# A third buffer for the second weight of a gate/up tile, queued for loading with the first

## The chip, the cores and the metric

The kernel runs on one core of one Trainium2 chip. Five engines work side by side, each through its own queue in order: TensorE (PE; its weight loads are shown apart as PEld), VectorE (DVE), ScalarE (ACT), GpSimd (POOL) and SyncE (SP), whose queue issues nearly all loads and stores. The metric is the device time in microseconds (us); lower is better.

## The reference

Two layers of an encoder on 512 tokens of width 1024: token mixing and memory attention, then a feed-forward part. The change is in the feed-forward part:

```python
h = rms_norm(x, g_ffn_pre[i])
gu = h @ w_gate_up[i]                       # 512 x 1024 by 1024 x 5632
f = (jax.nn.silu(gu[..., :D_FF]) * gu[..., D_FF:]) @ w_down[i]
x = x + rms_norm(f, g_ffn_post[i])
```

All of it is float32. D_FF is 2816.

## The kernel before

**Tiles and lots.** The gate/up product is worked in 22 tiles f = 0 to 21, each 128 columns of gate and the same 128 of up. `LOTS` cuts them into three lots: 0 to 7, 8 to 13, 14 to 21. After each lot the product with w_down for its tiles follows (`down`, after the third lot `ffn_out`). Tiles 0 and 1 are done in the plain way, the 20 others in seven products instead of eight, after Strassen's scheme in Winograd's form: sums of the activations' quarters (nS1, S2, S3, S4, made once) against sums of the weights.

**Weights of a tile.** A tile has two weights of 128 x 1024 float32, 512 KB each: raw (gate; pool `wraw`, 3 buffers, shared with all other weights) and rb (up; pool `gu`, 2 buffers). `prep_a` loads raw and splits it; `load_b` loads rb and makes two sums on VectorE: ru[:512] = raw[:512] + rb[:512] (L1043) and rb[:512] += rb[512:] (L1044). `prep_c` adds ru[512:] (L1049), `prep_d` adds to raw[512:] (L1056). Each of the four operands a (raw), c (ru), b (rb) and d (512 columns of raw) is then split into a high part on ScalarE (L313) and a low part on VectorE (L317), since each product is made of three matmuls of reduced precision. The 512-column split d is the last to read raw, so it frees the buffer for raw of tile f+3. The split b is the last to read rb, so it freed the buffer for rb of tile f+2.

**The order within a tile.** TensorE's order is written out by hand in `body(f)`: products with c (two), a of the next tile (first half), b (first half), a of the next tile (second half), b (second half), d. Each is 12 matmuls of 256 columns (L1065 to L1067). VectorE adds results that come back from the product banks: L1101 after the first b product, which must be done before the d product overwrites the bank; L1082 after the second a product; L1109 after the second b product; then L1115 and L1118 form the tile's output.

**The order on other engines.** Only TensorE's order is fixed by hand. For the other engines, and for the loads in SP's queue, a scheduler at build time takes instructions by their priority in the program and by the time at which it expects their inputs. Each engine then keeps that order on the chip, and waits at the head of its queue.

Of the kernel before, what the change touches and what calls it, by code (L numbers as in the profile page):

```python
# [9 lines left out]
F32 = mybir.dt.float32  # L10
# [6 lines left out]
P = 128  # L17
# [181 lines left out]
class Trunk:  # L199
# [791 lines left out]
    def ffn(self, l, pools, forms, late, done):  # L991
# [3 lines left out]
        nc = self.nc  # L995
        f32r = lambda pool, shape, tag, n=1: pool.tile(shape, F32R, tag=tag, name=tag, bufs=n)
        F, o, gu, tmp = {}, [], pools["gu"], None
        w, raw, st = {}, {}, {}

        def units(f):  # L1000
            w[f] = [self.unit(self.a["wgu"][l, f, b]) for b in range(2)]
# [23 lines left out]
        def pair(f, key, src, n=1024):  # L1025
            hi, lo = [self.whl.tile([P, 1024], F32R, tag=z, name=f"w{z}", bufs=4) for z in ("hi", "lo")]
            self.split(hi[:, :n], lo[:, :n], src)
            st[f][key] = (hi, lo)

        def prep_a(f):  # L1030
            st[f] = {}
            src = self.a["wgu"][l, f]
            ra = self.wraw.tile([P, 1024], F32, tag="raw", name="raw", bufs=3)
            nc.sync.dma_start(ra, src[0])
            raw[f] = ra
            pair(f, "a", ra)

        def load_b(f):
            src = self.a["wgu"][l, f]
            ru, rb = [gu.tile([P, 1024], F32, tag=z, name=z, bufs=2) for z in ("ru", "rb")]  # L1040
            nc.sync.dma_start(rb, src[1])
            with self.tc.issue_after(forms.last[1]) if f == 3 else nullcontext():
                nc.vector.tensor_add(ru[:, :512], raw[f][:, :512], rb[:, :512])  # L1043
                nc.vector.tensor_add(rb[:, :512], rb[:, :512], rb[:, 512:])  # L1044
            st[f].update(ru=ru, rb=rb)

        def prep_c(f):
            ru, rb = st[f]["ru"], st[f]["rb"]
# [36 lines left out]
        def body(f, pos, nxt, nxt2, fill):  # L1085
# [7 lines left out]
            if nxt is not None:  # L1093
                load_b(nxt)
                prep_c(nxt)
                p1(nxt)
            else:
                fill[0]()
# [7 lines left out]
            if nxt2 is not None:  # L1106
                prep_a(nxt2)
# [31 lines left out]
        for f in range(2):  # L1139
            for b in range(2):  # L1140
                plain(f, b, 1, pgs[f])
            act(f, pgs[f])
            if f == 0:
                forms.finish(0)
                prep_a(2)
                forms.finish(1)
        pools["forms"].close()

        for c, (f0, f1) in enumerate(LOTS):
            fs = list(range(f0, f1))  # L1150
# [2 lines left out]
            if c:  # L1153
                prep_a(gs[0])
            load_b(gs[0])
            prep_c(gs[0])
            prep_a(gs[1])
# [18 lines left out]
            if c < len(LOTS) - 1:  # L1176
                self.down(get, self.a["wd"][l], fs, c, o, head)
                if l == c == 0:
                    self.axial(gu.tile([P, 1024], F32, tag="ru", name="ru", bufs=2))
        done()  # L1180
        return get, fs, o, head

    def start(self, mkp):
# [215 lines left out]
```

## Time and profile before

| | us |
|---|---|
| median of 3 runs | 1095.49 |
| lowest, highest | 1094.43, 1097.13 |
| the profiled execution | 1097.01 |
| its span, first to last instruction | 1094.9 |
| TensorE busy | 1072.8 |
| VectorE busy | 840.8 |
| ScalarE busy | 659.1 |
| VectorE waits at L1043 for rb, for raw | 11.0, 12.0 |
| clock granted to TensorE (1 is full) | 0.998 |

A row of the timeline has the start (us from the span's start), the duration, the engine, the line, the operation, what it writes from what it reads, the count and, in brackets, the idle time before it and what ended that. "SPq" is a load or store issued by SP. A row of waits has the total, the number and the longest.

### The profile page before, as it was taken

The page shows a single profiled execution, that of the slowest core. Times are in us where ns is not written, and L with a number is a line of the kernel's source. Part 1 is how long each engine was busy: PE and PEld are TensorE (multiplying, and loading weights), DVE is VectorE, ACT ScalarE, POOL GpSimd, SP SyncE. Part 2 cuts the span into 40 slices and gives each one's busy share as a digit, 9 for nine tenths or more (in the row PEclk, how much of TensorE's full clock was granted, in tenths as well). Part 3 has the DMA queues.
Part 4 walks back from the last instruction along what each step waited for, and adds up shares of the span by engine and source line. Part 5 has one row for each costly group of instructions (what it writes and reads, how often), then busy time and mean ns, then how long its engine had stood idle before and what let it go on. Part 6 is the DMA issues. An engine that isn't in the chain of part 4 may idle for free.

```text
span 1094.9 us, 19518 instructions
## 1 busy us (share of the span) xinstructions
PE 1072.8 (98%) x7436; PEld 985.0 (90%) x7436; DVE 840.8 (77%) x1433; ACT 659.1 (60%) x1357; POOL 197.7 (18%) x341
## 2 busy tenths in 40 slices
PE   9999999999999999999999999999999999999997
PEld 7899878999889989998898888878999899899986
DVE  7889875999548867975888988758996478669854
ACT  7679874756445535653567888756664366346631
POOL 5773231102000000000444543312000000000001
PEclk9999999999999999999999999999999999999999
DMA  9621007344833472335533221144136123423243
GB/s 339 250 78 40 20 20 261 125 154 129 283 140 116 153 252 78 116 108 187 197 126 116 78 78 40 39 176 172 53 110 222 59 89 120 139 68 105 88 165 116
DMA packets 40702, 142.44 MB, mean 130 GB/s; under 512 B 4768, under 2 KB 5152, under 8 KB 40480
## 3 DMA queue, kind: packets, MB, share of 16 engines
q1 hardware_dynamic: 40320, 140.80, 37.4%
q8 instruction: 58, 0.95, 0.4%
q10 hardware_dynamic: 288, 0.40, 0.1%
q14 instruction: 36, 0.29, 0.1%
HBM read 122.30 MB, written 18.87 MB: 129 GB/s over the span
## 4 chain that ended last, share of the span: by engine, by line
PE 70%; DVE 5%; issue 2%; ACT 1%; POOL 1%; DMA 0%; DVEq 0%; POOLq 0%; ACTq 0%
PE ps L1065 11%; PE ps L1066 11%; PE ps L1067 11%; PE ps L304 10%; PE ps L303 10%; PE ps L305 10%; PE tp L668 2%; DVE wlo L317 1%; PE o L683 1%; PE o L682 1%; PE s L607 1%; PE s L608 1%; POOL r L337 1%; DVE hrows L317 1%; POOL p L658 0%
## 5 line engine op out<-in xcount | busy, mean ns | idle before, releaser
L313 ACT ACTIVATE whi<-raw 128x1024 fp32r<-128x1024 f32 (+3 forms) x206 | 169.2, 839 | 170.1 <-PE ps L1067 69.0
L317 DVE TENSOR_TENSOR wlo<-raw,whi 128x1024 fp32r<-128x1024 f32 (+3 forms) x202 | 191.0, 960 | 68.8 <-ACT whi L313 64.8
L1066 PE MATMUL ps<-hrows,wlo 128*128 128x256 f32 x640 | 176.4, 276 | 0.0
L1065 PE MATMUL ps<-hrows,whi 128*128 128x256 f32 x640 | 176.2, 275 | 0.0
L1067 PE MATMUL ps<-hrows,whi 128*128 128x256 f32 x640 | 176.2, 275 | 0.0
L303 PE MATMUL ps<-whi,hrows 128*128 128x256 f32 (+2 forms) x432 | 144.1, 333 | 0.0
L304 PE MATMUL ps<-wlo,hrows 128*128 128x256 f32 (+2 forms) x432 | 138.0, 320 | 1.6 <-DVE wlo L317 1.6
L304 PE MATMUL ps<-wlo,f 128*128 128x512 f32 (+1 forms) x360 | 138.6, 385 | 0.0
L303 PE MATMUL ps<-whi,f 128*128 128x512 f32 (+1 forms) x360 | 138.5, 385 | 0.0
L305 PE MATMUL ps<-whi,f 128*128 128x512 f32 (+1 forms) x360 | 138.5, 385 | 0.0
L305 PE MATMUL ps<-whi,hrows 128*128 128x256 f32 (+2 forms) x432 | 138.0, 320 | 0.0
L1065 PE MATMUL ps<-a,whi 128*128 128x256 f32 x480 | 132.3, 276 | 2.9 <-DVE c L1101 2.9
L1066 PE MATMUL ps<-a,wlo 128*128 128x256 f32 x480 | 132.1, 275 | 0.0
L1067 PE MATMUL ps<-a,whi 128*128 128x256 f32 x480 | 132.1, 275 | 0.0
L1066 PEld LDWEIGHTS ps<-hrows,wlo 128*128 128x128 f32 x640 | 120.1, 188 | 0.6
L1065 PEld LDWEIGHTS ps<-hrows,whi 128*128 128x128 f32 x640 | 120.1, 188 | 0.5
L1067 PEld LDWEIGHTS ps<-hrows,whi 128*128 128x128 f32 x640 | 120.1, 188 | 0.0
L346 POOL TENSOR_SCALAR e<-sso 128x1 f32<-128x1 f32 x8 | 3.4, 422 | 550.5 <-ACT junk L341 550.3
L658 POOL TENSOR_SCALAR p<-p,rd 128x256 f32<-128x256 f32 (+2 forms) x128 | 77.4, 623 | 102.5 <-DVE rd L655 62.3
L1065 PEld LDWEIGHTS ps<-a,whi 128*128 128x128 f32 x480 | 90.1, 188 | 3.5 <-DVE c L1101 3.3
L1066 PEld LDWEIGHTS ps<-a,wlo 128*128 128x128 f32 x480 | 90.1, 188 | 0.2
L1067 PEld LDWEIGHTS ps<-a,whi 128*128 128x128 f32 x480 | 90.1, 188 | 0.0
(201 smaller groups left out, 2551.0 us busy)
## 6 DMA issues: line engine op xcount, KB each, us to landing
raw<-in_wgu_dram SPq DMA_DIRECT2D x48, 512.0 KB, 4.4
raw<-in_wd_dram SPq DMA_DIRECT2D x44, 512.0 KB, 4.5
rb<-in_wgu_dram SPq DMA_DIRECT2D x40, 512.0 KB, 3.6
raw<-in_wo_dram SPq DMA_DIRECT2D x17, 512.0 KB, 4.1
raw<-in_wq_dram SPq DMA_DIRECT2D x16, 512.0 KB, 4.9
xt<-x SPq DMA_DIRECT2D x12, 512.0 KB, 4.9
raw<-in_wm_dram SPq DMA_DIRECT2D x8, 512.0 KB, 4.6
x<-y SPq DMA_DIRECT2D x8, 512.0 KB, 3.2
```

Source lines behind the costliest of these rows:

```text
L303: mm(out, lh, rh, start=first, stop=False)
L304: mm(out, lh, rl, start=False, stop=False)
L305: mm(out, ll, rh, start=False, stop=last)
L313: a = nc.scalar.activation(hi, src, AF.Copy)
L317: b = nc.vector.tensor_sub(lo, src, hi.bitcast(F32))
L337: g.tensor_tensor(r, r, self.mhalf[:, :r.shape[1]], op=OP.pow)
L607: nc.tensor.matmul(s[:, :n], qi, hd["ka"]()[:, k0 * P:k1 * P], start=True, stop=False)
L658: self.pooled = nc.gpsimd.tensor_scalar(hd["p"][z][:, :n], hd["p"][z][:, :n], rd[:, z:z + 1], 1.0, op0=OP.mult, op1=OP.mult)
L668: nc.tensor.transpose(tp[:, z], hd["p"][i][:, jj * P:(jj + 1) * P], self.ident)
L1065: mm(out, wh[:, s], rh, start=start and k == 0, stop=False, skip_group_check=True)
L1066: mm(out, wl[:, s], rh, start=False, stop=False, skip_group_check=True)
L1067: mm(out, wh[:, s], rl, start=False, stop=k == 3, skip_group_check=True)
```

## The change

The load of rb moves from `load_b` into `prep_a`, directly behind the load of raw. Every third tile, counted within a layer from tile 2, takes its rb from a new pool `gx` with one buffer, the others from `gu` as before, so there are three buffers in turn. The pool is opened when the temporary forms of the activations are closed, and closed at the end of the layer's last lot. The number and kind of instructions stay the same on each engine.

```diff
         F, o, gu, tmp = {}, [], pools["gu"], None
-        w, raw, st = {}, {}, {}
+        w, raw, st, turn, gx = {}, {}, {}, [-1], []
...
             raw[f] = ra
+            n = turn[0] = turn[0] + 1
+            rb = st[f]["rb"] = (gx[0] if n % 3 == 2 else gu).tile([P, 1024], F32, tag="rb", name="rb", bufs=1 if n % 3 == 2 else 2)
+            nc.sync.dma_start(rb, src[1])
             pair(f, "a", ra)
 
         def load_b(f):
-            src = self.a["wgu"][l, f]
-            ru, rb = [gu.tile([P, 1024], F32, tag=z, name=z, bufs=2) for z in ("ru", "rb")]
-            nc.sync.dma_start(rb, src[1])
+            ru, rb = gu.tile([P, 1024], F32, tag="ru", name="ru", bufs=2), st[f]["rb"]
             with self.tc.issue_after(forms.last[1]) if f == 3 else nullcontext():
                 nc.vector.tensor_add(ru[:, :512], raw[f][:, :512], rb[:, :512])
                 nc.vector.tensor_add(rb[:, :512], rb[:, :512], rb[:, 512:])
-            st[f].update(ru=ru, rb=rb)
+            st[f]["ru"] = ru
...
         pools["forms"].close()
+        extra = ExitStack()
+        gx.append(self.pool(extra, f"gx{l}"))
...
         done()
+        extra.close()
         return get, fs, o, head
```

TensorE's and GpSimd's orders are the same in both kernels; ScalarE's differs by one swap of neighbours in each layer. SP's and VectorE's differ at these places. In the new kernel lines from 1036 on stand one to four higher or lower: L1038 is the load of rb (L1041 before), L1044, L1045 and L1050 are the three sums (L1043, L1044 and L1049 before), L1057, L1083, L1102, L1110, L1116 and L1119 those that were L1056, L1082, L1101, L1109, L1115 and L1118. The numbers in names tell one tile's buffers from another's.

**SP at the start of layer 0's first lot**, before (raw_3305 and raw_3435 belong to tiles 3 and 4, rb_3511 to tile 4, rb_3641 to tile 5):

```order
L1034 DMA raw_3305<-in_wgu_dram 128x1024
L1034 DMA raw_3435<-in_wgu_dram 128x1024
L359 DMA gain_6460<-in_g_ffn_post_dram 128x1024
L359 DMA gain_6462<-in_g_mix_pre_dram 128x1024
L800 DMA xt_6644<-x00_74 128x1024
L800 DMA xt_6692<-x01_75 128x1024
L1041 DMA rb_3511<-in_wgu_dram 128x1024
L1034 DMA raw_3565<-in_wgu_dram 128x1024
L1041 DMA rb_3641<-in_wgu_dram 128x1024
```

The same place now (tile 4's rb is rb_3440, tile 5's is rb_3570, tile 6's is rb_3700):

```order
L1034 DMA raw_3308<-in_wgu_dram 128x1024
L1034 DMA raw_3438<-in_wgu_dram 128x1024
L1038 DMA rb_3440<-in_wgu_dram 128x1024
L1038 DMA rb_3570<-in_wgu_dram 128x1024
L1034 DMA raw_3568<-in_wgu_dram 128x1024
L1038 DMA rb_3700<-in_wgu_dram 128x1024
```

Each rb now stands one place of its kind earlier. The two gains and the two rows of x went to the end of layer 0's third lot, where the load of tile 21's rb stood; only there does the scheduler now find their memory free.

**VectorE in layer 0's first lot**, before: the sum of tile 5 (ru_3640), the split of tile 4's ru (ru_3510) and the result of tile 3 (c_3547), for which TensorE waits:

```order
L317 TENSOR_TENSOR wlo_3478<-raw_3305,whi_3477 128x512
L1044 TENSOR_TENSOR rb_3511<-rb_3511 128x512
L1118 SCALAR_TENSOR_TENSOR f12_3473<-s_3339,f02_3472 128x512
L1049 TENSOR_TENSOR ru_3510<-ru_3510,rb_3511 128x512
L1056 TENSOR_TENSOR raw_3435<-raw_3435,ru_3510 128x512
L1043 TENSOR_TENSOR ru_3640<-raw_3565,rb_3641 128x512
L317 TENSOR_TENSOR wlo_3517<-ru_3510,whi_3516 128x1024
L1101 TENSOR_TENSOR c_3547<-ps_3390,p5_3508 128x256
```

The same place now (tile 5's sum is ru_3645, tile 6's is ru_3775, tile 4's ru is ru_3515, tile 3's result is c_3550):

```order
L317 TENSOR_TENSOR wlo_3483<-raw_3308,whi_3482 128x512
L1050 TENSOR_TENSOR ru_3515<-ru_3515,rb_3440 128x512
L1119 SCALAR_TENSOR_TENSOR f12_3478<-s_3344,f02_3477 128x512
L1057 TENSOR_TENSOR raw_3438<-raw_3438,ru_3515 128x512
L317 TENSOR_TENSOR wlo_3520<-ru_3515,whi_3519 128x1024
L1044 TENSOR_TENSOR ru_3645<-raw_3568,rb_3570 128x512
L1102 TENSOR_TENSOR c_3550<-ps_3393,p5_3513 128x256
L1045 TENSOR_TENSOR rb_3570<-rb_3570 128x512
L1050 TENSOR_TENSOR ru_3645<-ru_3645,rb_3570 128x512
L1083 TENSOR_TENSOR s_3565<-ps_3552,p1_3536 128x256
L1044 TENSOR_TENSOR ru_3775<-raw_3698,rb_3700 128x512
```

The split of tile 4's ru went ahead of tile 5's sum, and tile 6's sum came forward into this tile's work.

**VectorE in layer 0's third lot**, before: from the 512-column split of tile 16 (raw_5527), which frees the buffer for raw of tile 19, to the sum of tile 18 (ru_5862):

```order
L317 TENSOR_TENSOR wlo_5700<-raw_5527,whi_5699 128x512
L1056 TENSOR_TENSOR raw_5657<-raw_5657,ru_5732 128x512
L1118 SCALAR_TENSOR_TENSOR f11_5695<-s_5524,f01_5694 128x512
L317 TENSOR_TENSOR wlo_5739<-ru_5732,whi_5738 128x1024
L1043 TENSOR_TENSOR ru_5862<-raw_5787,rb_5863 128x512
L1101 TENSOR_TENSOR c_5769<-ps_5612,p5_5730 128x256
```

The same place now, from the split of tile 16 (raw_5530) to the sum of tile 19 (ru_5997, from raw_5920):

```order
L317 TENSOR_TENSOR wlo_5705<-raw_5530,whi_5704 128x512
L1057 TENSOR_TENSOR raw_5660<-raw_5660,ru_5737 128x512
L1119 SCALAR_TENSOR_TENSOR f11_5700<-s_5527,f01_5699 128x512
L317 TENSOR_TENSOR wlo_5742<-ru_5737,whi_5741 128x1024
L1102 TENSOR_TENSOR c_5772<-ps_5615,p5_5735 128x256
L1044 TENSOR_TENSOR ru_5997<-raw_5920,rb_5922 128x512
```

The sum that stands behind tile 16's split is now that of tile 19, whose raw that split lets in; before it was that of tile 18. The result L1101 went ahead of it.

## The prediction

> **What bounds the kernel now.** I read the page's table of engines first, then the waits of TensorE, then the timelines of TensorE, VectorE and the load queue (SP) at the places those waits name.
>
> ```profile
> span 1094.9 us, 19518 instructions
> ...
> PE 1072.8 (98%) x7436; PEld 985.0 (90%) x7436; DVE 840.8 (77%) x1433; ACT 659.1 (60%) x1357; POOL 197.7 (18%) x341
> ```
>
> TensorE (PE) is busy for 98% of the span. Since a busy matmul may still be waiting inside its modelled duration, I look at a stretch of the gate/up work by itself, by windows; the columns are PE, weight loads, VectorE, ScalarE, GpSimd, clock, DMA share and GB/s:
>
> ```profile
> 418.00:490.00 72.00, 72.00 (x631) 71.72 (x630) 61.59 (x90) 44.64 (x75) 0.00 (x0) 1.00 0.33 107
> ```
>
> This is the third lot of layer 0. Weights are being loaded for 71.72 of 72 us, so there is nothing to win there: the loads already come in time for TensorE. VectorE works 61.59 of 72 us. Over the whole run, TensorE waits in a gate/up tile only here (total, times, longest):
>
> ```profile
> PE ps L1065 <- DVE c L1101: 2.9, 2, 2.3
> ```
>
> The two waits in TensorE's timeline, one in the first lot of each layer:
>
> ```profile
> 242.34 0.28 PE L1067 MATMUL ps<-hrows,whi 128*128 128x256 f32 x1
> 244.88 0.39 PE L1065 MATMUL ps<-a,whi 128*128 128x256 f32 x1 [2.27 <-DVE c L1101]
> ...
> 796.48 0.28 PE L1067 MATMUL ps<-hrows,whi 128*128 128x256 f32 x1
> 797.43 0.38 PE L1065 MATMUL ps<-a,whi 128*128 128x256 f32 x1 [0.67 <-DVE c L1101]
> ```
>
> Matmuls of this shape start 0.11 us apart, so 2.43 us are lost at 244.88 and 0.84 at 797.43: **3.3 us in all**. That is what a better supply of weights can bring.
>
> **What the change removes.** VectorE before the first wait, and the load queue:
>
> ```profile
> 229.03 0.69 DVE L1043 TENSOR_TENSOR ru<-raw,rb 128x512 f32<-128x512 f32 x1
> ...
> 239.86 0.69 DVE L1049 TENSOR_TENSOR ru<-ru,rb 128x512 f32<-128x512 f32 x1
> ...
> 242.66 0.69 DVE L1043 TENSOR_TENSOR ru<-raw,rb 128x512 f32<-128x512 f32 x1 [1.39 <-DMA rb<-in_wgu_dram]
> 243.28 1.22 DVE L317 TENSOR_TENSOR wlo<-ru,whi 128x1024 fp32r<-128x1024 f32 x1
> 244.41 0.42 DVE L1101 TENSOR_TENSOR c<-ps,p 128x256 f32<-128x256 f32 x1
> ```
>
> ```profile
> 220.83 0.33 SPq L359 DMA_DIRECT2D gain<-in_g_ffn_post_dram  x1
> ...
> 228.57 0.33 SPq L1041 DMA_DIRECT2D rb<-in_wgu_dram  x1
> ...
> 237.56 0.33 SPq L1041 DMA_DIRECT2D rb<-in_wgu_dram  x1
> ```
>
> The addition at 242.66 belongs to tile 5. It stands at the head of VectorE's queue and waits 1.39 us for rb of tile 5, asked for at 237.56 and landed 5.1 us later. Behind it stand the split of tile 4's ru and the addition L1101, for which TensorE waits. With the third buffer, rb of tile 4 is asked for directly behind raw of tile 4, ahead of the place where the gain load stood (220.83), and rb of tile 5 takes the place at 228.57. So this wait is gone.
>
> **What is late next in that lot** is VectorE itself. Spacings come from a steady tile of the third lot:
>
> ```profile
> 452.13 0.68 DVE L1043 TENSOR_TENSOR ru<-raw,rb 128x512 f32<-128x512 f32 x1
> 452.73 0.42 DVE L1101 TENSOR_TENSOR c<-ps,p 128x256 f32<-128x256 f32 x1
> 453.07 0.68 DVE L1044 TENSOR_TENSOR rb<-rb 128x512 f32<-128x512 f32 x1
> 453.67 0.69 DVE L1049 TENSOR_TENSOR ru<-ru,rb 128x512 f32<-128x512 f32 x1
> 454.27 0.42 DVE L1082 TENSOR_TENSOR s<-ps,p 128x256 f32<-128x256 f32 x1
> 454.80 1.23 DVE L317 TENSOR_TENSOR wlo<-raw,whi 128x1024 fp32r<-128x1024 f32 x1
> 455.94 0.42 DVE L1109 TENSOR_TENSOR c<-ps,u 128x256 f32<-128x256 f32 x1
> 456.28 1.22 DVE L317 TENSOR_TENSOR wlo<-rb,whi 128x1024 fp32r<-128x1024 f32 x1
> 457.41 0.69 DVE L1115 TENSOR_TENSOR s<-s,c 128x512 f32<-128x512 f32 x1
> 458.01 0.69 DVE L317 TENSOR_TENSOR wlo<-raw,whi 128x512 fp32r<-128x512 f32 x1
> ```
>
> So one start follows the next after 0.60 us for 512 columns, 0.33 for 256 and 1.13 for a split of 1024. From the addition of tile 3 (229.03, unmoved) to L1101 of tile 3, the new order has 13 operations of 512 columns, 3 of 256 and 4 of 1024: 7.8 + 1.0 + 4.5 = 13.3 us. L1101 starts at about 242.4, ends 0.42 later, and TensorE goes on at about 242.9, 2.0 us earlier than before. It could have gone on at 242.45, so 0.45 us of the stall stay. The next tile brings a small one: from L1101 of tile 3 to that of tile 4 stand 9 operations of 512, 3 of 256 and 3 of 1024, 5.4 + 1.0 + 3.4 = 9.8 us, against 9.5 us of matmuls (below), since additions of later tiles now stand earlier. That costs 0.3. **Gain in layer 0: 1.7 us.** The same count in layer 1:
>
> ```profile
> 782.95 0.68 DVE L1043 TENSOR_TENSOR ru<-raw,rb 128x512 f32<-128x512 f32 x1
> ...
> 796.96 0.42 DVE L1101 TENSOR_TENSOR c<-ps,p 128x256 f32<-128x256 f32 x1
> ```
>
> 782.95 + 13.3 = 796.25 instead of 796.96, so 0.7 us, less the same 0.3: **gain in layer 1: 0.4 us.** Together 2.1; the ends are 3.3 (no stall stays) and 1.0 (each stall that stays is half a microsecond longer than counted).
>
> **What the change adds.** It adds no instruction; every load and every addition is there as often as before. But VectorE's order moves: the addition L1043 of a tile now stands nearly one tile earlier, right behind the split that frees the buffer for its other input. That input is raw, the first weight, which keeps its three buffers: raw of tile f is asked for when the 512-column split of tile f-3 has read the buffer. Before, that split was followed by a whole tile of work ahead of the addition that needs the new raw; now four instructions lie between. Three loads of the third lot before:
>
> ```profile
> 419.78 0.33 SPq L1034 DMA_DIRECT2D raw<-in_wgu_dram  x1
> ...
> 448.00 0.33 SPq L1041 DMA_DIRECT2D rb<-in_wgu_dram  x1
> 449.21 0.33 SPq L1034 DMA_DIRECT2D raw<-in_wgu_dram  x1
> ...
> 458.73 0.33 SPq L1034 DMA_DIRECT2D raw<-in_wgu_dram  x1
> ```
>
> The landing times of the five such loads in this lot, then of those in the same lot of layer 1:
>
> ```profile
> DMA to landing us min/median/max: 4.1/4.4/4.4
> ```
>
> ```profile
> DMA to landing us min/median/max: 4.2/4.4/6.1
> ```
>
> A tile takes 9.52 us (449.21 to 458.73). The new circle is: L1043 of tile f, then L1044, L1082, L1049, the raw split, L1109, the rb split, L1115 and the 512-column split (0.60 + 0.60 + 0.33 + 0.60 + 1.13 + 0.33 + 1.13 + 0.60 + 0.69 = 6.0 us), then the issue and the landing of raw of tile f+1 (4.35), then L1043 of tile f+1: **10.4 us, against 9.52.** So VectorE falls behind by 0.9 us a tile while the circle lasts, from tile 17 to tile 21. L1043 of tile 17 goes as soon as its raw lands, at 419.78 + 4.4 = 424.2; L1101 comes between in the first round, so tile 21's goes at 424.2 + 10.7 + 3 x 10.4 = 466.1. Behind it come L1044, L1082, L1049 (with itself 2.1 us) and then the split of raw of tile 20, done 1.23 later, at 469.5. Before, that split and the matmul that needs it:
>
> ```profile
> 464.32 1.22 DVE L317 TENSOR_TENSOR wlo<-raw,whi 128x1024 fp32r<-128x1024 f32 x1
> ```
>
> ```profile
> 468.58 0.28 PE L1066 MATMUL ps<-a,wlo 128*128 128x256 f32 x1
> ```
>
> There was a slack of 3.0 us; now the matmul waits 0.9. After tile 21 no addition of this kind follows and VectorE catches up. With landings of 4.1 the stall is 0; with 4.4 it is 1.1; with one landing of 6.1, as once in layer 1, it is 2.8. I take 0.9 in layer 0 and 1.1 in layer 1, near the medians: **loss 2.0.** The first and second lots have only two rounds of the circle each and end before the slack is used up: I count 0, at most 0.4 each.
>
> **What else moves.** In layer 0 the gain vectors and two rows of x for the end of the feed-forward are loaded at the end of the third lot, where the last rb load stood, and not at 220.83.
>
> ```profile
> 467.04 0.33 SPq L1041 DMA_DIRECT2D rb<-in_wgu_dram  x1
> ```
>
> ```profile
> 512.01 0.69 DVE L940 TENSOR_TENSOR o<-o,gain 128x512 f32<-128x512 f32 x1 [0.19 <-ACT junk L341]
> ```
>
> The first use of a gain is 45 us after that place, so four loads cost nothing unless they hold up w_down's loads behind them. Those wait for VectorE to free raw buffers anyhow.
>
> **Two rules of the Trainium skill.** Its page "Perfetto Trace Analysis", section "Optimization Strategy", says that the same gap coming back on the engine that should be saturated can mean too few buffers for the next tile; by that rule alone the third buffer would win the whole 3.3 us. The rows here show two gaps and no recurring one, so the rule hardly fits. Its page "DMA: Bandwidth & Descriptors", section "Rules for kernel authors", advises to issue a load early and to wait for it late, by which the change would also gain 3.3 us. The order of instructions here does only half of it: rb is issued a tile earlier, and VectorE's wait for both weights moves a tile earlier too.
>
> **The sum.** -2.1 + 2.0 = -0.1 us. The profiled execution took 1097.01 us, 1.5 above the median of 1095.49 (its span, 1094.9, leaves 2.1 outside); the sum is taken off the median: **1095.4 us**. About 3.3 us (0.3%) is what a measurement of this kernel can tell from no change.
>
> **The rivals.**
> - All stalls go and none comes: raw lands in 4.1 us or less, and VectorE's order costs nothing. 1095.5 - 3.3 = 1092.2. For it: one raw landed in 4.1. Against: the medians, and VectorE's 13.3 us of queued work in the first lot. Chance 0.12, half of it beyond 0.3%. The two rules of the Trainium skill above, "Optimization Strategy" of "Perfetto Trace Analysis" and "Rules for kernel authors" of "DMA: Bandwidth & Descriptors", lead to this rival.
> - The circle through raw becomes the bound: in both layers raw lands later than 4.4, since the deeper rb load runs beside it. It decides from 4.2 us on and costs four steps of the excess in each third lot. At 5.0 us the step is 11.05, tile 21's addition is 2.6 us later than counted, and the stall is 3.5 us in each layer: 7.0 - 2.1 = +4.9, 1100.4; at 4.7 it is +2.5. For it: one landing of 6.1. Against: an rb load starts 1.2 us ahead of the raw load in each tile before (448.00 and 449.21) and after alike. Chance 0.16, most of it beyond 0.3%.
> - The change does not do what it says, the third buffer being held by its earlier tenants: 1095.5. Against: the order has that load directly behind the raw loads. Chance 0.06.
> - The forecast, within 2.5 us of the median either way: 0.66.
>
> So faster by over 0.3%: 0.06, within 0.3%: 0.80, slower: 0.14. The range from 1092.4 to 1099.0 takes in the first rival and part of the second.
>
> **What would show it.** The additions L1043 of the whole run, with their idle time at the end:
>
> ```profile
> L1043 DVE TENSOR_TENSOR ru<-raw,rb 128x512 f32<-128x512 f32 x40 | 27.5, 687 | 23.1 <-DMA raw<-in_wgu_dram 12.0 <-DMA rb<-in_wgu_dram 11.0
> ```
>
> Right: the wait of L1065 for L1101 at 244.88 falls from 2.3 to below 0.6 us; VectorE's L1043 waits for raw and no longer for rb (its waits before stand at the end of the row above), in the third lots by about 1 to 1.5 us a tile; TensorE shows a new wait near 468 for the split of raw, about 1 us. Wrong: no new wait there, which means that raw landed sooner; or a wait in each tile from 440 on, which means that the slack was smaller; or a wait for a gain or a w_down split after 470.

## The result, and the profile after

| | us |
|---|---|
| the changed kernel, median of 4 runs | 1104.38 |
| lowest, highest | 1103.61, 1104.91 |
| the old kernel beside it, median of 4 runs | 1096.31 |
| ratio, 95% interval | 1.0073 [1.0053, 1.0093] |
| the profiled execution, its span | 1104.53, 1102.4 |

The changed kernel is slower by 0.7%, about 8 us; 1095.4 was forecast, and the time lies above the range. Two executions of the experiments took far longer than the others of their kernels, 2176.94 us in e1, where it was the profiled one, and 1181.25 us in e6, and the ratios leave them out. The page of the changed kernel: the span, the busy time of the engines, then the chain that ended last, by engine and by line.

```profile
span 1102.4 us, 19508 instructions
...
PE 1077.4 (98%) x7436; PEld 987.8 (90%) x7436; DVE 841.4 (76%) x1433; ACT 655.5 (59%) x1357; POOL 195.7 (18%) x341
...
PE 80%; DVE 9%; ACT 4%; DMA 3%; issue 2%; POOL 2%; DVEq 0%; POOLq 0%; ACTq 0%
PE ps L304 13%; PE ps L303 13%; PE ps L305 13%; PE ps L1067 10%; PE ps L1066 10%; PE ps L1068 9%; PE tp L668 3%; DMA raw<-in_wgu_dram 3%; DVE wlo L317 2%; PE o L682 2%; PE o L683 2%; PE s L607 1%; PE s L608 1%; PE ps L513 1%; DVE mT L331 1%
```

The work is the same (7436 matmuls, 1433 VectorE instructions), the span is 7.5 us longer, and a load of raw now stands in the chain. Since TensorE's instructions are the same in the same order, the time from one of them to another can be compared by their starts. A lot below runs from the first matmul of its first product in seven parts to the first matmul of the w_down product behind it; the 12 matmuls of w_down within the last tile count with the lot. The third lot of layer 0 in the changed kernel, its first and last row in TensorE's timeline:

```profile
412.66 0.28 PE L1066 MATMUL ps<-a,whi 128*128 128x256 f32 x1
...
495.94 0.39 PE L303 MATMUL ps<-whi,f 128*128 128x512 f32 x1
```

That is 83.28 us. The same for all stretches, in us, with three kernels of the experiments beside it (the first stretch starts at the first matmul):

| stretch | old | changed | changed, second profile | e1: sums late | e2: four raw | e5: first lots only |
|---|---|---|---|---|---|---|
| up to the first lot | 220.8 | 219.2 | 219.6 | 219.4 | 219.7 | 219.6 |
| layer 0, first lot | 62.61 | 61.07 | 61.28 | 61.01 | 60.90 | 61.13 |
| layer 0, second lot | 60.00 | 60.40 | 60.55 | 60.03 | 59.99 | 60.00 |
| layer 0, third lot | 79.09 | 83.28 | 81.94 | 79.07 | 79.27 | 79.03 |
| between the layers | 281.5 | 281.9 | 281.8 | 281.7 | 281.4 | 281.8 |
| layer 1, first lot | 61.24 | 61.05 | 61.36 | 60.99 | 60.89 | 61.03 |
| layer 1, second lot | 60.01 | 61.91 | 62.33 | 60.03 | 60.05 | 60.00 |
| layer 1, third lot | 79.05 | 82.82 | 83.45 | 79.07 | 79.07 | 79.03 |

The w_down products between the lots take 40.83 and 29.95 us in each of these profiles. So the first lots gained 1.54 + 0.19 = 1.7 us, and the second and third lots lost 0.4 + 4.2 + 1.9 + 3.8 = 10.3. The rest (-1.6 ahead of the first lot, +0.4 between the layers, +0.2 behind the last lot) lies in work that the change doesn't touch. The first stretch varies by itself: in e3, whose queues have the old kernel's order, it took 219.2.

The waits of the changed kernel that answer to those of before (total, times, longest):

```profile
DVE ru L1044 <- DMA raw<-in_wgu_dram: 40.0, 23, 4.7
...
PE ps L1067 <- DVE wlo L317: 5.4, 7, 2.0
...
PEld ps L1066 <- DVE c L1102: 0.7, 4, 0.2
```

VectorE's sum (L1043 before, L1044 now) waits for raw 23 times, 40.0 us in all, and no longer for rb. TensorE's matmuls no longer wait for the result c (only weight loads still do, 0.7 us in all), and a wait for a split has come. One round of VectorE in the third lot of layer 0, from one sum to the next:

```profile
432.68 0.69 DVE L1044 TENSOR_TENSOR ru<-raw,rb 128x512 f32<-128x512 f32 x1 [1.62 <-DMA raw<-in_wgu_dram]
433.41 0.69 DVE L1045 TENSOR_TENSOR rb<-rb 128x512 f32<-128x512 f32 x1
...
438.15 0.69 DVE L317 TENSOR_TENSOR wlo<-raw,whi 128x512 fp32r<-128x512 f32 x1
...
441.30 0.42 DVE L1102 TENSOR_TENSOR c<-ps,p 128x256 f32<-128x256 f32 x1
443.44 0.69 DVE L1044 TENSOR_TENSOR ru<-raw,rb 128x512 f32<-128x512 f32 x1 [1.72 <-DMA raw<-in_wgu_dram]
...
455.50 0.69 DVE L1044 TENSOR_TENSOR ru<-raw,rb 128x512 f32<-128x512 f32 x1 [3.02 <-DMA raw<-in_wgu_dram]
...
466.15 0.69 DVE L1044 TENSOR_TENSOR ru<-raw,rb 128x512 f32<-128x512 f32 x1 [1.61 <-DMA raw<-in_wgu_dram]
```

The loads of raw in SP's queue in the same stretch:

```profile
438.87 0.33 SPq L1034 DMA_DIRECT2D raw<-in_wgu_dram  x1
...
449.63 0.33 SPq L1034 DMA_DIRECT2D raw<-in_wgu_dram  x1
...
461.68 0.33 SPq L1034 DMA_DIRECT2D raw<-in_wgu_dram  x1
```

The circle of the prediction can be read off: the sum at 432.68, the split that frees the buffer at 438.15 (ends 438.84), the load at 438.87, the next sum at 443.44. That is 6.19 us of VectorE and 4.57 of load, 10.76 in all, against TensorE's 9.52. The round behind it takes 12.06, because that load, issued at 449.63, serves its sum only at 455.50. The chain of waits goes through the same circle near the end of the lot (its rows have start, duration, what), and a round earlier, behind the late load, stands TensorE's longest stall of the lot:

```profile
460.37 0.69 DVE s L1116
461.06 0.61 DVE wlo L317
461.68 4.35 DMA raw<-in_wgu_dram
466.15 0.70 DVE ru L1044
...
468.51 1.15 DVE wlo L317
469.70 0.39 PE ps L1067
```

```profile
459.04 0.39 PE L1067 MATMUL ps<-a,wlo 128*128 128x256 f32 x1 [1.98 <-DVE wlo L317]
...
469.70 0.39 PE L1067 MATMUL ps<-a,wlo 128*128 128x256 f32 x1 [0.59 <-DVE wlo L317]
```

### The profile page after: what moved, and what is told of

It is laid out like the page before. It is cut to its first block, busy times and chain, and to the rows that moved or that the text cites. A ratio compares the mean times of both kernels' runs of the same rounds, so it can differ in the third digit from the quotient of the medians.

```text
span 1102.4 us, 19508 instructions
## 1 busy us (share of the span) xinstructions
PE 1077.4 (98%) x7436; PEld 987.8 (90%) x7436; DVE 841.4 (76%) x1433; ACT 655.5 (59%) x1357; POOL 195.7 (18%) x341
## 4 chain that ended last, share of the span: by engine, by line
PE 80%; DVE 9%; ACT 4%; DMA 3%; issue 2%; POOL 2%; DVEq 0%; POOLq 0%; ACTq 0%
PE ps L304 13%; PE ps L303 13%; PE ps L305 13%; PE ps L1067 10%; PE ps L1066 10%; PE ps L1068 9%; PE tp L668 3%; DMA raw<-in_wgu_dram 3%; DVE wlo L317 2%; PE o L682 2%; PE o L683 2%; PE s L607 1%; PE s L608 1%; PE ps L513 1%; DVE mT L331 1%
## 5 line engine op out<-in xcount | busy, mean ns | idle before, releaser
L1067 PE MATMUL ps<-hrows,wlo 128*128 128x256 f32 x640 | 177.6, 277 | 0.0
L1067 PE MATMUL ps<-a,wlo 128*128 128x256 f32 x480 | 133.6, 278 | 5.5 <-DVE wlo L317 5.4
L1067 PEld LDWEIGHTS ps<-hrows,wlo 128*128 128x128 f32 x640 | 120.2, 188 | 0.8 <-DVE wlo L317 0.2
L1067 PEld LDWEIGHTS ps<-a,wlo 128*128 128x128 f32 x480 | 90.2, 188 | 7.2 <-DVE wlo L317 7.0
```

What stands on the lines that cost most here:

```text
L1067: mm(out, wl[:, s], rh, start=False, stop=False, skip_group_check=True)
```

## The experiments

Theory A: the loss comes from the early sum at the head of VectorE's queue, which waits for raw, and raw waits for a buffer that VectorE itself frees. Against it stand B (the loads, queued together or moved, cost by themselves) and D (the early sums crowd VectorE, whatever they wait for). In the experiments' timelines the sum is L1045, one line lower, unless said otherwise. Ratios are to the old kernel, run on the same chip in the same session.

**e1, the sums in their old place, the loads in their new one.** An ordering edge keeps a tile's first sum behind the split of the tile before's ru:

```diff
-            self.split(hi[:, :n], lo[:, :n], src)
+            st[f][key + "lo"] = self.split(hi[:, :n], lo[:, :n], src)[1]
...
+            prev = st.get(f - 1, {}).get("clo")
-            with self.tc.issue_after(forms.last[1]) if f == 3 else nullcontext():
+            with self.tc.issue_after(forms.last[1]) if f == 3 else self.tc.issue_after(prev) if prev is not None else nullcontext():
```

> The changed kernel with one edit: the sum ru[:512] = raw[:512] + rb[:512] of a tile is ordered behind the split of the tile before's ru, where the old kernel has it. The load queue keeps the new order in every row, the third buffer stays. Theory A (VectorE's head of queue: the sum stands a tile early and waits for raw, which comes only after its own circle): the waits for raw split in the third lots and in layer 1's second lot go (lot times back to 79.1, 60.0 and 79.05 us from 83.3, 61.9 and 82.8), the gain of 1.5 us in layer 0's first lot stays; about 1094.5 us, 10 below the changed kernel. Theory B (the load queue: rb loaded earlier runs beside raw and delays it, or the moved gain and x rows do): nothing but the wait at the sum changes, the third lots stay near 83 us and the time near 1104.

Measured: 1094.2 us, ratio 0.9976 [0.9968, 0.9985]. B falls: SP's order is the changed kernel's in every row, and the loss is gone. A second run of this kernel gave the profile that is compared here:

> The changed kernel with the sums in their old place once more, for its profile. Theory A: third lots 79.1 us, second lots 60.0, first lot of layer 0 61.0 to 61.3; VectorE's waits for raw at the sum as few as in the old kernel (7 or fewer, 12 us or less, against 23 and 40), while rb and raw are loaded in the new order and raw's landing stays near 4.4 us. Theory B: raw's landing is what costs, and third lots above 81 us show it in this profile too.

It took 1093.8 us, and its stretches stand in the table. The waits in its profile:

```profile
DVE ru L1045 <- DMA raw<-in_wgu_dram: 9.3, 4, 3.6
```

A load, and the sums after it, in its third lot of layer 0 (SP, then VectorE):

```profile
436.69 0.33 SPq L1034 DMA_DIRECT2D raw<-in_wgu_dram  x1
```

```profile
439.62 0.68 DVE L1045 TENSOR_TENSOR ru<-raw,rb 128x512 f32<-128x512 f32 x1
...
449.14 0.68 DVE L1045 TENSOR_TENSOR ru<-raw,rb 128x512 f32<-128x512 f32 x1
```

The sums are 9.52 us apart again and wait for nothing. The load at 436.69 is that of the next tile: it has until 449.14, 12.45 us, where in the changed kernel the sum that needs it is the next one, four instructions behind. Raw lands hardly faster than in the changed kernel: over the sixteen loads of the second and third lots of both layers it takes 4.50 us on average in this profile, 4.65 in the changed kernel and 4.53 in the old one. It is waited for later.

**e2, a fourth buffer for raw, the sums still early.**

```diff
-            ra = self.wraw.tile([P, 1024], F32, tag="raw", name="raw", bufs=3)
+            n = turn[0] = turn[0] + 1
+            q = n % 4 == 3
+            ra = (gx[1] if q else self.wraw).tile([P, 1024], F32, tag="raw", name="raw", bufs=1 if q else 3)
...
-            n = turn[0] = turn[0] + 1
...
-        gx.append(self.pool(extra, f"gx{l}"))
+        gx.extend(self.pool(extra, f"gx{z}{l}") for z in range(2))
```

> The changed kernel with a fourth buffer for raw in the gate/up tiles, in turn; sums stay a tile early. Theory A (the circle from the 512-column split through the issue and landing of raw to the next sum): raw is now asked for a tile (9.5 us) earlier, the circle has 19 us for two tiles, and VectorE's waits for raw in the third lots fall from 1.5 to 4.6 us a tile to under 0.5; third lots near 79.2 us, about 1094 to 1096 us. Theory D (not the wait: the early sums push VectorE's splits and results back by their own 1.8 us a tile): the third lots stay above 81 us and the time above 1100.

Measured: 1093.33 us, ratio 0.9965 [0.9954, 0.9977], below what either theory expected and the lowest ratio of all, though its interval overlaps those of e1 and e9. Three rows of its third lot, a load of raw and two sums:

```profile
427.48 0.33 SPq L1036 DMA_DIRECT2D raw<-in_wgu_dram  x1
```

```profile
430.53 0.69 DVE L1045 TENSOR_TENSOR ru<-raw,rb 128x512 f32<-128x512 f32 x1
...
440.04 0.69 DVE L1045 TENSOR_TENSOR ru<-raw,rb 128x512 f32<-128x512 f32 x1
```

The load at 427.48 is for the sum at 440.04, a whole tile later than in the changed kernel, and no sum of the third lots' rounds waits, though each still stands a tile early. The early place alone costs nothing, which goes against D; what the changed kernel lacks is raw in time.

**e5, the new form in the first lots only.** Tiles 8 to 21 load rb in `load_b`, into the two old buffers.

```diff
-            rb = st[f]["rb"] = (gx[0] if n % 3 == 2 else gu).tile([P, 1024], F32, tag="rb", name="rb", bufs=1 if n % 3 == 2 else 2)
-            nc.sync.dma_start(rb, src[1])
+            if f < 8:
+                rb = st[f]["rb"] = (gx[0] if n % 3 == 2 else gu).tile([P, 1024], F32, tag="rb", name="rb", bufs=1 if n % 3 == 2 else 2)
+                nc.sync.dma_start(rb, src[1])
...
-            ru, rb = gu.tile([P, 1024], F32, tag="ru", name="ru", bufs=2), st[f]["rb"]
+            ru = gu.tile([P, 1024], F32, tag="ru", name="ru", bufs=2)
+            if f < 8:
+                rb = st[f]["rb"]
+            else:
+                rb = st[f]["rb"] = gu.tile([P, 1024], F32, tag="rb", name="rb", bufs=2)
+                nc.sync.dma_start(rb, self.a["wgu"][l, f][1])
```

> The changed kernel with the new form (third buffer, rb asked for with raw) in the first lot of each layer only; tiles 8 to 21 load rb in the old place into the two old buffers. Theory A: first lots as in the changed kernel (61.1 us each), second and third lots as before (60.0, 79.1); 1096.3 - 1.7 = about 1094.5. Theory B' (the loss in the third lots is set by what stands ahead of them, such as the pool held open through the layer or the moved loads of gains and x rows): the third lots stay above 81 us although their own tiles are unchanged, about 1101.

Measured: 1094.82 us, ratio 0.9984 [0.9976, 0.9993]. The gain of the first lots stays and the later lots are as before, though the pool is open through the whole layer and the gain vectors are loaded in another place.

**The changed kernel once more.**

> The changed kernel once more, for a second profile beside these runs. Theory A: the same lots lose (third lots of both layers, second lot of layer 1), rounds of VectorE's sum from 10.6 us up, each set by 6.2 us of VectorE's work plus the landing of raw; which tile loses most moves with single landings of 5 to 6 us. Chance alone (the first profile had two odd landings): third lots near 80 to 81 us and about 1098.

Measured: 1105.6 us, ratio 1.008 [1.0063, 1.0098]. The same four lots lose (10.1 us together, table). In layer 0's third lot no load came late this time, its rounds took 10.56 to 11.14 us, and it still lost 2.9 us, where it had lost 4.2. Layer 1's second and third lots lost more than in the first profile.

**e10, the extra buffer given to raw alone.** The old kernel with a fourth raw buffer and two of rb:

```diff
-            ra = self.wraw.tile([P, 1024], F32, tag="raw", name="raw", bufs=3)
+            n = turn[0] = turn[0] + 1
+            q = n % 4 == 3
+            ra = (gx[0] if q else self.wraw).tile([P, 1024], F32, tag="raw", name="raw", bufs=1 if q else 3)
...
+        extra = ExitStack()
+        gx.append(self.pool(extra, f"gx{l}"))
...
+        extra.close()
```

> The old kernel with the extra buffer given to raw (a fourth) and none to rb; the sums stay in their old place in the second and third lots but for three of them. Theory A: nothing early waits, so nothing is lost (third lots 79.1, second lots 60.0); rb of tile 5 is still asked for only when the rb split of tile 3 is done, so most of the wait at the result of tile 3 in layer 0's first lot stays: 1095 to 1096.9. Theory E (the extra 4 KB a partition or the loads of gain and x moved by it cost time by themselves): above 1100.

Measured: 1096.1 us, ratio 0.9996 [0.9988, 1.0005], as expected by A. The wait in the first lot is still there in its profile (here L1067 is the first of a product's three matmuls and L1103 the result c):

```profile
PE ps L1067 <- DVE c L1103: 2.4, 2, 1.9
```

So a buffer more costs nothing by itself, nor do the moved loads of gain and x. The gain of e2 needs both: rb's third buffer against the old wait, and raw's fourth against the new.

**e3, the load moved, no third buffer.**

```diff
-            rb = st[f]["rb"] = (gx[0] if n % 3 == 2 else gu).tile([P, 1024], F32, tag="rb", name="rb", bufs=1 if n % 3 == 2 else 2)
+            rb = st[f]["rb"] = gu.tile([P, 1024], F32, tag="rb", name="rb", bufs=2)
```

> The load of rb moved into prep_a, but with the two old buffers and no third. The built order is the old one in every row of each engine, since a load waits for its buffer before it is ready. Every theory: as the old kernel within 0.15%, 1095 to 1098, with third lots of 79.1 us; a difference would mean that something other than the order of instructions counts. Its first part, up to the first lot, shows by how much profiles of the same work differ there (219.2 to 220.8 us so far).

Measured: 1096.19 us beside 1097.35, ratio 0.9997 [0.9987, 1.0006]. Where the load stands in the program does nothing; the buffer is what moves both the load and the sum. In this profile layer 0's first lot took 64.0 us, with the old order of instructions, against 62.6 in the profile of before: the old stall varies by more than a microsecond between executions.

**e6, raw in two loads.** The sum needs only the first 512 columns of raw:

```diff
-            nc.sync.dma_start(ra, src[0])
+            for z in range(2):
+                nc.sync.dma_start(ra[:, 512 * z:512 * z + 512], src[0][:, 512 * z:512 * z + 512])
```

> The changed kernel with the load of raw cut into two loads of 512 columns (256 KB each), the first half first. The early sum reads only the first half. Theory A (round = 6.2 us of VectorE's work plus issue and landing of what the sum reads): the first half lands about 1 us sooner than all of raw, the round falls from 10.7 to about 9.7 against TensorE's 9.5, four rounds cost 0.8 of a slack of 3.0, so the losses of the second and third lots go: about 1094.5 to 1096 us. If the sum waits for both halves, the second issue adds 0.4 a round and the third lots lose 1.6 more each: about 1108. Theory D (the landing is not in the round, the early sums cost by VectorE's order): stays near 1104.

Measured: 1098.53 us, ratio 1.0016 [1.0005, 1.0028], above A's range and below D's number. Its timelines, two loads and the sums around them (a row of two issues has x2):

```profile
427.63 0.80 SPq L1035 DMA_DIRECT2D raw<-in_wgu_dram  x2
...
437.73 0.80 SPq L1035 DMA_DIRECT2D raw<-in_wgu_dram  x2
```

```profile
431.27 0.69 DVE L1045 TENSOR_TENSOR ru<-raw,rb 128x512 f32<-128x512 f32 x1 [0.99 <-DMA raw<-in_wgu_dram]
...
441.38 0.69 DVE L1045 TENSOR_TENSOR ru<-raw,rb 128x512 f32<-128x512 f32 x1 [1.14 <-DMA raw<-in_wgu_dram]
```

From issue to sum it is 3.64 us instead of 4.57, and the round falls from 10.76 to 10.11, not to 9.7: in the order built for it the result c is back behind the sum, which makes VectorE's part 6.46. So the landing of raw is a term of the round, as A says, but the size expected was wrong. The second lots are back at 60.00 us, layer 0's third lot at 80.81; layer 1's third lot stays at 82.62, with one round of 11.59.

**e8, each early sum made twice.**

```diff
-                nc.vector.tensor_add(ru[:, :512], raw[f][:, :512], rb[:, :512])
+                for _ in range(2):
+                    nc.vector.tensor_add(ru[:, :512], raw[f][:, :512], rb[:, :512])
```

> The changed kernel with the sum ru[:512] = raw[:512] + rb[:512] made twice in a row (the second writes the same), 40 additions of 0.6 us or 24 us of VectorE more. In the order built from it ru[512:] moves behind the 512-column split, so between a sum and the split that lets the next raw in stand sum, sum, L1083, L1045, raw split, L1110, rb split, L1116, split: 6.0 us, as in the changed kernel. Theory A (only what stands between the sum and that split is in the round; the rest of the tile lies beside raw's landing): no change, third lots 82 to 84 us, 1103 to 1106. Theory D (VectorE's work of a whole tile sets the round): each round 0.6 longer, third lots 2.4 and second lots 1.2 longer each, about 1111.

Measured: 1112.47 us, ratio 1.0145 [1.0132, 1.0158]: a miss for A in the total, and near D's 1111. By lots it is another matter. The third lots take 84.03 and 83.45 us, 0.7 and 0.6 more than in the changed kernel, near A's 82 to 84 and not the 2.4 more of D. A round there is 11.0 (one pair of sums and the next, with their waits):

```profile
437.33 1.42 DVE L1045 TENSOR_TENSOR ru<-raw,rb 128x512 f32<-128x512 f32 x2 [1.63 <-DMA raw<-in_wgu_dram]
...
448.34 1.42 DVE L1045 TENSOR_TENSOR ru<-raw,rb 128x512 f32<-128x512 f32 x2 [1.57 <-DMA raw<-in_wgu_dram]
```

The five sums of layer 0's third lot stand 44.40 us apart in all, exactly as in the changed kernel: the extra 0.6 us a tile lies beside raw's landing there. The first lots, where VectorE has a backlog and hardly waits for raw, rose to 62.61 and 62.22 us, and the second to 61.69 and 63.74. In the second lots the first round starts 0.6 and 0.4 us later than in the changed kernel, and the two rounds take 0.3 and 1.0 us longer; the cause of this was not taken apart. So VectorE's total work does count in the first lots, where it isn't hidden by the wait; for the second lots that is not shown.

**e9, third rb buffer, fourth raw buffer and late sums together.** The edits of e1 and e2.

> The third rb buffer, a fourth raw buffer and the sums in the old place behind the split of the tile before's ru. Theory A: neither load is waited for at the head of VectorE's queue in a steady tile; same as with four raw buffers alone, 1093.3 within 0.7, third lots 79.1. If the early sums still cost something with four raw buffers, it is up to 1 us faster than that.

Measured: 1094.24 us, ratio 0.9975 [0.9965, 0.9985], 0.2 us above the range expected and not below e2. With four raw buffers the early sums cost nothing that this shows.

## Why the prediction was wrong, step by step

- **The gain: right.** 1.7 us were counted in layer 0's first lot and 1.54 came, 1.33 in the second profile; in layer 1 0.4 were counted and 0.2 came, and none in the second profile. TensorE's matmuls no longer wait for the result c. That the number came so near is partly luck, since the old stall varies by more than a microsecond (e3).
- **The mechanism of the loss: right.** The sum waits for raw and not for rb, the circle runs over the operations that were named, and TensorE waits at the split of raw, in the lots' later tiles: 0.59 us at the matmul that the prediction named, and 1.98 a tile earlier, behind the late load.
- **The size of the round: wrong, and this is the step that failed.** The prediction put a round at 6.0 of VectorE and 4.35 of load, 10.4 us. The four rounds of layer 0's third lot took 10.93, 10.76, 12.06 and 10.65 (sums at 421.75 and 466.15: 44.40 in all, where 10.7 + 3 x 10.4 = 41.9 was counted). In layer 1 the five sums stand 44.18 us apart. Two terms were too small. VectorE's part is 6.19 instead of 6.0 (with c between, in the first round of a lot, 6.46), mostly because L1045, directly behind the sum, starts 0.73 us after it and not 0.60; in the old kernel's steady tile the result c stood between the two. And issue to sum, over the 16 loads of the four lots that lost, is 4.77 on average instead of 4.35. Thirteen of them lie between 4.3 and 4.8, three between 5.4 and 6.0. Of the 4.77, 4.65 are the landing and 0.12 lie between the landing and the start of the sum. The prediction put that at nothing: it reads the 5.1 us from issue to sum of tile 5's rb as the landing, which was 5.01.
- **The slack turned a small error into a large one.** A round too long by 0.6 us, four times, is 2.5 us, and the first 3.0 us of delay had been paid for by the slack already. With the measured rounds the prediction's own sum gives 0.9 + 2.5 = 3.4 us in layer 0's third lot and 0.9 + 2.3 = 3.2 in layer 1's; 4.2 and 3.8 were lost. In layer 0's lot TensorE's rows show 2.6 of the 4.2 as waits; the rest are small delays before, at and behind these places, which were not taken apart.
- **The second lots: wrong.** They were counted at 0, at most 0.4. Layer 0's stayed at 0.4 (0.55 in the second profile). In layer 1's, one late load made a round of 12.41, the two rounds took 23.04 us against 19.04 of TensorE's, and 4.0 is more than the slack: 1.9 us lost, 2.3 in the second profile. The three sums of that lot:

```profile
888.71 0.69 DVE L1044 TENSOR_TENSOR ru<-raw,rb 128x512 f32<-128x512 f32 x1 [0.77 <-DMA raw<-in_wgu_dram]
...
901.12 0.69 DVE L1044 TENSOR_TENSOR ru<-raw,rb 128x512 f32<-128x512 f32 x1 [3.10 <-DMA raw<-in_wgu_dram]
...
911.75 0.69 DVE L1044 TENSOR_TENSOR ru<-raw,rb 128x512 f32<-128x512 f32 x1 [1.59 <-DMA raw<-in_wgu_dram]
```

- **The moved loads of gain and x: right**, nothing (e1, e5, e10).
- **The sum** should have read -1.7 + 10.3 and not -2.1 + 2.0. The second rival, "the circle through raw becomes the bound", is what happened, but not for its reason, a landing delayed by the deeper rb load: the mean landing over the sixteen loads was 4.65 us, against 4.53 before. That its 3.5 us a lot came near is in part luck, and it left out the second lots. In the circle each landing adds to the next, so the mean with its late ones counts and not a median: with the 4.53 that the old profile holds, the prediction's sum would have given 0.9 + 4 x 0.18 = 1.6 us a lot. The rest of the error lies in VectorE's part and in the start of the sum behind the landing.

What the rows say of the two rules of the Trainium skill: e1, with the load early and the wait late, gains 2.7 us, and the changed kernel, with both early, loses 8. So the advice of "DMA: Bandwidth & Descriptors", section "Rules for kernel authors", to issue a load early and to wait for it late, agrees with the runs in both of its halves; the change had kept only the first. In the changed kernel VectorE's wait of 1.5 us or more came back with each round of the third lots (1.62, 1.72, 3.02 and 1.61 in layer 0's), and a fourth raw buffer removed it (e2). The page "Perfetto Trace Analysis", section "Optimization Strategy", says that such a recurring gap can mean too few buffers; it speaks of the engine that should be saturated, but here it fits VectorE, which isn't, and the buffer that was short was not the one that the change added.

## What to carry to other kernels

A buffer more for one input of an operation lets the scheduler bring the whole operation forward, and then it waits, at the head of its engine's queue, for the other input. Before adding a buffer, follow the circle of every input: work from the use to the instruction that frees the buffer, plus issue, plus landing, against the time of a tile; where it is longer, deepen that input too (e2) or hold the use in its old place (e1). In such a circle take the mean time from issue to use, with its late ones, and not the median landing, and remember that slack is spent over several tiles before anything shows.

## What the runs showed of the hardware that was not expected

Within the lots, late landings of raw come together with loads of code. In the changed kernel's profile, the DMA view of the stretch with the late load (issued at 449.63, queues with packets and MB, then the issues with their landing):

```profile
q1 hardware_dynamic: 288, 1.05, 47.1%
q8 instruction: 1, 0.02, 0.8%
...
raw<-in_wgu_dram SPq DMA_DIRECT2D x1, 512.0 KB, 5.8
```

And the same of the round before, without a packet of the instruction queue:

```profile
q1 hardware_dynamic: 288, 1.05, 55.3%
...
raw<-in_wgu_dram SPq DMA_DIRECT2D x1, 512.0 KB, 4.5
```

Take the loads of raw that were issued within the lots, over ten profiles of this study (the old kernel, the changed one twice, e1's second run, e2, e3, e5, e8, e9 and e10). Of 95 that had a packet of an instruction queue under way within 4.2 us of their issue, 12 took 5.2 us or more to land, up to 6.2; of 119 without one, none did (the longest took 4.8). Outside the lots this doesn't hold: of the same ten profiles' loads of raw for gate/up tiles there, 13 of 116 with such a packet and 55 of 150 without one took 5.2 us or more, so something else delays those. One packet of 0.02 MB beside 512 KB looks too small to matter, and most loads with it were on time. That the code load is the cause is not shown: the two only come together, and no run here took the code load away.
